# Second layer: values of all three groups for the first half of the tokens ahead of the keys

## The chip, the cores and the metric

The kernel runs on one core of one Trainium2 chip. The metric is device time in microseconds (us), the median of several runs. Engines: TensorE (PE) multiplies matrices, VectorE (DVE), ScalarE (ACT) and GpSimd (POOL) do the elementwise work, SyncE (SP) issues the DMAs. Every engine works through its own queue in order.

## The reference

Two layers over 1024 tokens of width 1024, batch 1, in float32. The first is gated linear attention; its output goes through a layer norm and gives `x1`. The second is attention with three dilated windows (groups) over one shared set of keys and values. What matters here:

```python
def shared_kv(x, w_kv):                  # x is x1, (1, 1024, 1024)
    kv = x @ w_kv
    k, v = jnp.split(kv, [SWA_KV_HALF], axis=-1)
    k = rope(k.reshape(bsz, s, 6, 128), pos)     # 3 groups x 2 heads, rotated by position
    v = v.reshape(bsz, s, 3, 2, 128)
...
x = layer_norm(DEEPNORM_ALPHA * x + y, ln_g[layer], ln_b[layer])   # mean, variance, scale, shift
```

The queries are projected the same way and rotated. Each group then attends within its own window and stride, and the three results are mixed by their softmax weights.

## The kernel before

Everything is kept transposed: 128 features on the partitions, 1024 tokens along the free axis, cut into two halves of 512 tokens. Float32 products are made of three matmuls in a rounded format: each operand is split into a high part (`xh`, `wh`) and a low part (`xl`, `wl`), and `mm3` (L616) adds `wh xh`, `wh xl` and `wl xh`. ACT rounds the high part (`split_hi`), DVE or POOL subtracts to get the low part (`split_lo`).

Weights come through `load_w` (L603): a DMA into `wf` (2 buffers), then `wh` (3 buffers) and `wl` (3 buffers), up to 1024 columns each. Accumulators `acc` have two banks.

`project` (L633) makes one 128-feature piece for one or both halves: 24 matmuls of 512 columns a half (8 slices of the input, three matmuls each). `project_tok` (L642) makes 256 features token by token: it needs two weight pieces, and works in blocks of 128 tokens, each 24 matmuls of 256 columns; the first 12 use the first weight piece, the others the second. The values of a group are made this way, four blocks a half.

Before the second layer starts, `out_ln(0, half)` (L1017) makes `x1` for each half: projection, residual (`rt`), sum over features by ones-matmuls on PE (`ms<-sum,onesr`), subtraction of the mean, squares (`sq`), the second pair of column sums, the scale factor `R` by ACT, then for each of eight slices a product with `R`, a scaling and shift, and the split into `x1h` and `x1l`. The second half's projection is still on PE while the first half is normalised, and the second half is normalised while PE already works for the second layer.

`layer_b` (L1124) starts the second layer. Its order is at L1201 to L1217: values of group 0 for the first half; the six key pieces for the first half; the same six for the second half (weights loaded again), each followed by `rows`, which turns a slice of `x1` with four PE transposes for the end of the program; values of group 0 for the second half; then values of group 1 and of group 2 for all tokens. Each key half piece is rotated on DVE by `rope` (L1134): a product with the cosines (`t<-acc,cosT`), two with the sines, and an addition into `K` (DVE or POOL). Values of groups 1 and 2 go to DRAM (`Vn`, `vd`) and come back in another order (`load_v`). Then query projection and attention follow, head by head.

The text order is not the issue order. `Sched.order` (L249) simulates the program with a cost table and lists, for each engine, the operation that can start first; among equals the one written first wins, with weight loads moved ahead and evacuations of accumulators a little ahead. The order that results is fixed at build time.

Of the kernel before, what the change touches and what calls it, by code (L numbers as in the profile page):

```python
# [575 lines left out]
def trunk(tc, xT, wP, wA, wAv, wa, w2, b2, ng, wO, wK, wV, wB, wOB, lng, lnb,  # L576
# [19 lines left out]
    def page(pool, dt, name):  # L596
        return pool.tile([128, T], dt, name=name, tag="pg", bufs=16)

    def hs(half):
        return slice(half * 512, half * 512 + 512)  # L600


    def load_w(src):  # L603
        with S.later(-WEIGHTS):
            return load_w_now(src)
# [21 lines left out]
    def proj_cols(w, xs, r, acc):  # L627
        hi, lo = w
        for kt in range(NK):
            xh, xl = xs[kt]  # L630
            mm3(acc, hi[:, kt, :], lo[:, kt, :], xh[:, r], xl[:, r], kt)

    def project(piece, xs, evac, halves=(0, 1)):  # L633
        w = load_w(piece)
        for half in halves:
            acc = ps.tile([128, 512], F32, name="acc", bufs=2)
            proj_cols(w, xs, hs(half), acc)
            with S.later(-EVAC):
                evac(half, acc)


    def project_tok(unit, xs, blocks, evac):  # L642
        w = [load_w(unit[:, kh * 4:kh * 4 + 4, :]) for kh in range(2)]
        for j, sel in blocks:
            acc = ps.tile([128, 256], F32, name="acc", bufs=2)
            for kt in range(NK):
                hi, lo = w[kt // 4]
                xh, xl = xs[kt]
                wh, wl = hi[:, kt % 4, :], lo[:, kt % 4, :]
                with S.group():  # L650
                    S.tensor.matmul(acc, sel(xh), wh, start=(kt == 0), stop=False)
                    S.tensor.matmul(acc, sel(xh), wl, start=False, stop=False)
                    S.tensor.matmul(acc, sel(xl), wh, start=False, stop=(kt == NK - 1))
            with S.later(-EVAC):
                evac(j, acc)

    def turn_blocks(dst, blocks):

        n = len(blocks)
        pt = ps.tile([128, 4, 128], F32, name="ms", bufs=2)  # L660
        with S.group():
            for i, b in enumerate(blocks):
                S.tensor.transpose(pt[:, i, :], b, ident)
        S.va.copy(dst, pt[:, :n, :].rearrange("p a b -> p (a b)"))

    def blk(x, j):
        return x[:, j * 128:j * 128 + 128]
# [335 lines left out]
    def small(name, tag, bufs, dt=F32, shape=(128, 512)):  # L1003
        return hp.tile(list(shape), dt, name=name, tag=tag, bufs=bufs)
# [108 lines left out]
    def to_group(pg, g, half):  # L1113
        if g == 2:
            return pg.rearrange("p (e a n) -> p n a e", e=16, a=8)[:, half * 4:half * 4 + 4]
        n = 512 // DIL[g]
        return pg.rearrange("p (r i) -> p i r", r=DIL[g])[:, half * n:half * n + n, :]

    def tok_view(ap, g):
        if g == 2:  # L1120
            return ap.rearrange("p (n a e) -> p n a e", n=4, a=8)
        return ap.rearrange("p (i r) -> p i r", r=DIL[g])

    def layer_b(xs):  # L1124
# [9 lines left out]
        def rope(pg, g, half, acc):  # L1134
            r = hs(half)
            t1 = small("t1", "t1", 2)
            S.vector.tensor_mul(t1, acc, cosT[:, r])
            t2 = small("t2", "t2", 2)
            S.vector.tensor_mul(t2[0:64, :], acc[64:128, :], sinT[64:128, r])
            S.vector.tensor_mul(t2[64:128, :], acc[0:64, :], sinT[0:64, r])  # L1140
            S.vp.tensor_add(to_group(pg, g, half), tok_view(t1, g), tok_view(t2, g))

        K = [[page(p0, F32, f"K{c}{g}") for g in range(3)] for c in range(2)]
        V = [[None] * 3 for _ in range(2)]

        def proj_v0(blocks):
            for c in range(2):
                if V[c][0] is None:
                    V[c][0] = page(p0, F32, f"V{c}0")

            def evac(j, acc):
                S.scalar.activation(blk(V[0][0], j), acc[:, 0:128], AF.Copy)
                S.vector.tensor_copy(blk(V[1][0], j), acc[:, 128:256])
            project_tok(wV[0], xs, [(j, lambda x, j=j: blk(x, j)) for j in blocks], evac)


        def proj_v(g):
            stage = {}

            def evac(j, acc):  # L1160
                if j % 4 == 0:
                    stage[j // 4] = page(p0, F32, "Vn")
                pg = stage[j // 4]
                dst = pg[:, j % 4 * 256:j % 4 * 256 + 256]
                if j % 2:
                    S.scalar.activation(dst, acc, AF.Copy)
                else:
                    S.vector.tensor_copy(dst, acc)
                if j % 4 == 3:
                    h = j // 4 * 512  # L1170
                    rows = pg.rearrange("p (n e) -> p n e", n=4)
                    if g == 1:
                        S.sync.dma_start(vd[h:h + 512, :].rearrange("(n p) e -> p n e", p=128), rows)
                    else:
                        for c in range(2):
                            S.sync.dma_start(vd3[c][h:h + 512, :].rearrange("(n p) e -> p n e", p=128),
                                              rows[:, :, c * 128:c * 128 + 128])
            project_tok(wV[g], xs, [(j, lambda x, j=j: blk(x, j)) for j in range(8)], evac)

        def load_v(c, g):  # L1180
            V[c][g] = page(p0, F32, f"V{c}{g}")
            if g == 1:
                for n in range(2):
                    S.sync.dma_start(
                        V[c][g].rearrange("p (r n e) -> p r n e", r=4, n=2)[:, :, n, :],
                        vd[n * 512:n * 512 + 512, c * 128:c * 128 + 128].rearrange("(p r) e -> p r e", r=4))
            else:

                src = vd3[c].rearrange("(n a s k j) e -> k s a n (j e)", n=8, a=8, s=2, k=2)
                for k in range(2):  # L1190
                    for s in range(2):
                        S.sync.dma_start(V[c][g][k * 64:k * 64 + 64, s * 512:s * 512 + 512], src[k, s])

        def rows(et):
            f, t = small("x1f", "d", 4), small("x1r", "d", 4)
            S.sync.dma_start(f, x1d[et][:, 512:1024])
            turn_blocks(t, [blk(f, i) for i in range(4)])
            for i in range(4):
                S.sync.dma_start(x1t[i][:, et * 128:et * 128 + 128], blk(t, i))

        proj_v0(range(4))  # L1201
        for half in range(2):
            for g in range(3):
                for c in range(2):
                    project(wK[2 * g + c], xs, lambda hf, acc, p=K[c][g]: rope(p, g, hf, acc), (half,))
                    if half:
                        rows(2 * g + c)
        proj_v0(range(4, 8))
        rows(6)
        rows(7)  # L1210
        proj_v(1)
        load_v(0, 1)
        proj_v(2)
        load_v(0, 2)
        for g in range(3):
            S.sync.dma_start(kvd[g], K[1][g])
        S.sync.dma_start(kvd[3], V[1][0])  # L1217
# [252 lines left out]
    for half in range(2):  # L1470
        out_ln(0, hs(half), lambda et: load_w(wO[et]), lambda et: xT[et * 128:et * 128 + 128, :], emit_a)
    U = layer_b(x1s)

    ogs.clear()
# [118 lines left out]
```

## Time and profile before

| | |
|---|---|
| median of 3 runs | 1194.42 us (1194.0 to 1195.4) |
| the profiled execution | 1194.93 us, of which the trace's span is 1193.1 us |
| PE | busy 1173.8 us (98%) |
| DVE | busy 760.7 us (64%) |
| ACT | busy 477.4 us (40%) |
| POOL | busy 191.9 us (16%) |

The span is the time from the first to the last recorded instruction; the remaining 1.8 us lie around it. A matmul counts as busy from its start to its modelled end, and matmuls overlap, so the distance between the starts of two neighbours (the pitch) tells more than the duration. All times in the rows are counted from the span's start.

### The profile page before, as it was taken

What the parts mean: (1) busy time and instruction counts of PE and PEld (TensorE: products, weight loads), DVE (VectorE), ACT (ScalarE), POOL (GpSimd) and SP (SyncE); (2) the same over time, 40 slices, a digit from 0 to 9 for tenths busy, and PEclk for the clock granted to TensorE, in tenths of its full rate; (3) what the DMA queues carried; (4) which work ended last, traced back from release to release, by engine and by line L of the source; (5) the groups of instructions that cost most, each with busy time, mean ns of one, the idle gap of its engine ahead of it and who ended that gap; (6) DMA issues with size and microseconds to landing.
All of it is one profiled execution on the core that took longest, in us unless ns stands there. A gap on an engine that the chain in (4) does not pass through costs nothing.

```text
span 1193.1 us, 20435 instructions
## 1 busy us (share of the span) xinstructions
PE 1173.8 (98%) x8220; PEld 1006.7 (84%) x8220; DVE 760.7 (64%) x1448; ACT 477.4 (40%) x1000; POOL 191.9 (16%) x126
## 2 busy tenths in 40 slices
PE   9999999999999998999999999999999999999997
PEld 7898988988988887879988888888888888888885
DVE  6482962953977598972155747565746675747578
ACT  5352533534454344332115352525244336345242
POOL 0011101211222122331010302020203022203000
PEclk9999999999999999999999999999999999999999
DMA  8102111121243454375231111121242110224544
GB/s 258 51 20 71 37 55 53 38 70 37 70 168 101 138 199 135 133 213 177 89 107 37 39 52 37 37 54 36 55 142 40 52 38 19 55 73 125 172 145 176
DMA packets 93232, 107.52 MB, mean 90 GB/s; under 512 B 44017, under 2 KB 62321, under 8 KB 93137
## 3 DMA queue, kind: packets, MB, share of 16 engines
q1 hardware_dynamic: 93136, 106.22, 28.4%
q8 instruction: 64, 1.05, 0.4%
q14 instruction: 32, 0.25, 0.1%
HBM read 85.02 MB, written 21.17 MB: 89 GB/s over the span
## 4 chain that ended last, share of the span: by engine, by line
PE 92%; DVE 5%; issue 1%; ACT 1%; DMA 1%; SPq 0%; POOL 0%; DVEq 0%; ACTq 0%; POOLq 0%
PE acc L441 66%; PE po L441 10%; PE lv L441 9%; PE ms L441 4%; PE pro L441 3%; DVE X L441 2%; DVE t L441 1%; DVE oT L441 1%; DMA xf<-in_xT 1%; DVE rt L441 0%; DVE K L441 0%; ACT wh L441 0%; DVE b L441 0%; DVE sum L441 0%; DVE x1l L441 0%
## 5 line engine op out<-in xcount | busy, mean ns | idle before, releaser
L441 PE MATMUL acc<-x1h,wh 128*128 128x512 f32 x608 | 251.8, 414 | 1.7 <-DVE t L441 1.7
L441 PE MATMUL acc<-x1l,wh 128*128 128x512 f32 x608 | 238.0, 391 | 0.2 <-DVE x1l L441 0.2
L441 PE MATMUL acc<-x1h,wl 128*128 128x512 f32 x608 | 238.1, 392 | 0.0
L441 ACT ACTIVATE wh<-wf 128x1024 fp32r<-128x1024 f32 (+2 forms) x102 | 106.1, 1042 | 265.4 <-PE acc L441 201.1
L441 POOL TENSOR_TENSOR wl<-wf,wh 128x1024 fp32r<-128x1024 f32 x45 | 108.0, 2400 | 607.2 <-ACT wh L441 573.5
L441 PEld LDWEIGHTS acc<-x1h,wl 128*128 128x128 f32 x608 | 114.6, 189 | 24.7
L441 PEld LDWEIGHTS acc<-x1h,wh 128*128 128x128 f32 x608 | 114.9, 189 | 24.0 <-DVE t L441 2.4
L441 PEld LDWEIGHTS acc<-x1l,wh 128*128 128x128 f32 x608 | 115.0, 189 | 22.2 <-DVE x1l L441 0.8
L441 DVE TENSOR_TENSOR wl<-wf,wh 128x1024 fp32r<-128x1024 f32 (+2 forms) x57 | 74.2, 1301 | 64.7 <-ACT wh L441 64.3
L441 ACT ACTIVATE P<-P,sts 128x128 f32<-128x128 f32 (+2 forms) x192 | 81.2, 425 | 45.1 <-DVE sts L441 44.2
L441 DVE TENSOR_TENSOR t<-acc,cosT 128x512 f32<-128x512 f32 x60 | 41.4, 690 | 71.4 <-PE acc L441 71.3
L441 DVE TENSOR_TENSOR t<-acc,sinT 64x512 f32<-64x512 f32 x120 | 82.6, 688 | 1.8 <-ACT R L441 0.2
L441 PE MATMUL acc<-xh,wh 128*128 128x512 f32 x208 | 82.5, 397 | 0.0
L441 PE MATMUL acc<-xh,wl 128*128 128x512 f32 x208 | 81.1, 390 | 0.0
L441 PE MATMUL acc<-xl,wh 128*128 128x512 f32 x208 | 81.0, 389 | 0.0
L441 PE MATMUL acc<-wh,xh 128*128 128x256 f32 x256 | 75.6, 295 | 0.0
L441 DVE TENSOR_TENSOR Q<-t,t 128x512 f32<-128x512 f32 x48 | 71.4, 1488 | 1.6
L441 DVE CUSTOM_DVE_ANT_0 P<-lv,bmask 128x256 f32<-128x256 f32 (+1 forms) x128 | 47.5, 381 | 39.0 <-PE lv L441 37.9
L441 PE MATMUL acc<-wl,xh 128*128 128x256 f32 x256 | 72.3, 282 | 0.0
L441 PE MATMUL acc<-wh,xl 128*128 128x256 f32 x256 | 72.3, 282 | 0.0
L441 PE MATMUL lv<-K,Q 128*64 128x64 f32 (+2 forms) x512 | 68.3, 286 | 0.0
L441 PE MATMUL po<-PT,V 64*128 64x64 f32 (+2 forms) x592 | 68.2, 293 | 0.0
(229 smaller groups left out, 2351.6 us busy)
## 6 DMA issues: line engine op xcount, KB each, us to landing
wf<-in_wB SPq DMA_DIRECT2D x32, 512.0 KB
wf<-in_wO SPq DMA_DIRECT2D x16, 512.0 KB
wf<-in_wOB SPq DMA_DIRECT2D x16, 512.0 KB
wf<-in_wA SPq DMA_DIRECT2D x13, 512.0 KB
wf<-in_wK SPq DMA_DIRECT2D x12, 512.0 KB
wf<-in_wAv SPq DMA_DIRECT2D x8, 512.0 KB
res<-in_xT SPq DMA_DIRECT2D x16, 256.0 KB
wf<-in_wV SPq DMA_DIRECT2D x8, 512.0 KB
```

The costliest lines, as they stand in the source:

```text
L441: getattr(handle[o.eng], meth)(*[conv(a) for a in args], **{k: conv(v) for k, v in kw.items()})
```

## The change

`proj_v` takes a half, so that groups 1 and 2 are made in two calls. The first half of the tokens now has its values of all three groups made first. Then each key piece is made for both halves from one weight load, followed by `rows`. Then come the values of groups 1 and 2 for the second half, `rows(6)` and `rows(7)`, and the values of group 0 for the second half.

```diff
-        def proj_v(g):
+        def proj_v(g, half):
...
-            project_tok(wV[g], xs, [(j, lambda x, j=j: blk(x, j)) for j in range(8)], evac)
+            project_tok(wV[g], xs, [(j, lambda x, j=j: blk(x, j)) for j in range(half * 4, half * 4 + 4)], evac)
...
         proj_v0(range(4))
-        for half in range(2):
-            for g in range(3):
-                for c in range(2):
-                    project(wK[2 * g + c], xs, lambda hf, acc, p=K[c][g]: rope(p, g, hf, acc), (half,))
-                    if half:
-                        rows(2 * g + c)
-        proj_v0(range(4, 8))
+        for g in (1, 2):
+            proj_v(g, 0)
+        for g in range(3):
+            for c in range(2):
+                project(wK[2 * g + c], xs, lambda hf, acc, p=K[c][g]: rope(p, g, hf, acc))
+                rows(2 * g + c)
+        for g in (1, 2):
+            proj_v(g, 1)
+            load_v(0, g)
         rows(6)
         rows(7)
-        proj_v(1)
-        load_v(0, 1)
-        proj_v(2)
-        load_v(0, 2)
+        proj_v0(range(4, 8))
```

PE, the second pair of column sums (`ms<-sum,onesr`, the variance of the second half). `acc` is an accumulator, `x1h0` to `x1h7` are the high parts of the eight slices of `x1`, the numbers behind an underscore count buffers. Before:

```order
L441 MATMUL acc_4782<-x1h7_4583,wh_4720 128x512
L441 MATMUL acc_4782<-x1l7_4597,wh_4720 128x512
L441 MATMUL acc_4782<-x1h7_4583,wl_4734 128x512
L441 MATMUL ms_4838<-sum_4828,onesr_193 128x512
L441 MATMUL ms_4838<-sum_4832,onesr_193 128x512
L441 MATMUL acc_4848<-x1h0_4416,wh_4740 128x512
```

And now:

```order
L441 MATMUL acc_4876<-wh_4861,x1h4_4502 128x256
L441 MATMUL acc_4876<-wl_4874,x1h4_4502 128x256
L441 MATMUL acc_4876<-wh_4861,x1l4_4517 128x256
L441 MATMUL ms_4903<-sum_4869,onesr_193 128x512
L441 MATMUL ms_4903<-sum_4888,onesr_193 128x512
L441 MATMUL acc_4876<-wh_4861,x1h5_4533 128x256
```

The sums stood behind the second key half piece; they now stand 15 matmuls into the first block of the values of group 2.

DVE, from the low split of that sum (`sum<-sq2,sum`) to the first slices of the layer norm's end. `t1` and `t2` are the rotary products, `rt` the rows that are normalised, `R` their scale factor. Before:

```order
L441 TENSOR_TENSOR t1_4826<-acc_4782,cosT_4553 128x512
L441 TENSOR_TENSOR sum_4832<-sq2_4700,sum_4828 128x512
L441 TENSOR_TENSOR t2_4836<-acc_4736,sinT_4557 64x512 x2
L441 TENSOR_TENSOR K00_4846<-t1_4787,t2_4836 128x512
L441 TENSOR_TENSOR t2_4852<-acc_4782,sinT_4557 64x512 x2
L441 TENSOR_TENSOR K10_4861<-t1_4826,t2_4852 128x512
L441 TENSOR_TENSOR rt_4242<-rt_4242,R_4844 128x512
L441 TENSOR_SCALAR rt_4242<-rt_4242,lngc_124,lnbc_128 128x512
```

And now:

```order
L441 COPY Vn_4780<-acc_4806 128x256
L441 TENSOR_TENSOR wl_4874<-wf_4750,wh_4861 128x1024
L441 TENSOR_TENSOR sum_4888<-sq2_4700,sum_4869 128x512
L441 TENSOR_TENSOR wl_4896<-wf_4782,wh_4880 128x1024
L441 COPY Vn_4925<-acc_4876 128x256
L441 TENSOR_TENSOR rt_4242<-rt_4242,R_4919 128x512
L441 TENSOR_SCALAR rt_4242<-rt_4242,lngc_124,lnbc_128 128x512
```

The rotary steps are gone from this part of the queue; value copies and weight splits stand there. The first rotary step now stands behind the last product with `R`.

PE, the first matmuls that read the second half of `x1`. Before, they open the second round of key pieces (`acc_5015`, the first piece again), behind all six first-half pieces (`acc_4973` is the sixth):

```order
L441 MATMUL acc_4973<-x1h7_4583,wh_4892 128x512
L441 MATMUL acc_4973<-x1l7_4597,wh_4892 128x512
L441 MATMUL acc_4973<-x1h7_4583,wl_4909 128x512
L441 MATMUL acc_5015<-x1h0_4416,wh_4937 128x512
L441 MATMUL acc_5015<-x1l0_4424,wh_4937 128x512
```

Now they follow the first half of the first key piece (`acc_5028`), with the same weights:

```order
L441 MATMUL acc_5028<-x1h7_4583,wh_4880 128x512
L441 MATMUL acc_5028<-x1l7_4597,wh_4880 128x512
L441 MATMUL acc_5028<-x1h7_4583,wl_4896 128x512
L441 MATMUL acc_5077<-x1h0_4416,wh_4880 128x512
L441 MATMUL acc_5077<-x1l0_4424,wh_4880 128x512
```

Between the end of the second half's projection and this place PE has three value units and one key half piece, where it had one value unit and six key half pieces. From the query projection on, every engine's order is what it was.

## Rows read from the trace of the kernel before

**Rows 1.** The page, part 2: PE's busy tenths in 40 equal slices.
```profile
PE   9999999999999998999999999999999999999997
```

**Rows 2.** PE timeline, 448 to 598: start, duration, operation, [idle before <-releaser].
```profile
448.71 0.28 PE L441 MATMUL acc<-wh,x1h 128*128 128x256 f32 x1
...
455.90 0.90 PE L441 MATMUL ms<-sum,onesr 128*128 128x512 f32 x2
456.64 0.28 PE L441 MATMUL acc<-wh,x1h 128*128 128x256 f32 x1
...
460.96 0.40 PE L441 MATMUL acc<-x1h,wh 128*128 128x512 f32 x1
...
471.64 0.39 PE L441 MATMUL acc<-x1h,wl 128*128 128x512 f32 x1
473.47 0.49 PE L441 MATMUL ms<-sum,onesr 128*128 128x512 f32 x1 [1.44 <-ACT sum L441]
475.92 0.80 PE L441 MATMUL ms<-sum,onesr 128*128 128x512 f32 x1 [1.96 <-DVE sum L441]
477.35 0.79 PE L441 MATMUL acc<-x1h,wh 128*128 128x512 f32 x1 [0.63 <-DVE t L441]
...
482.12 0.39 PE L441 MATMUL acc<-x1h,wl 128*128 128x512 f32 x1
...
504.13 0.60 PE L441 MATMUL ms<-ident,x1f 128*128 128x128 f32 x4
504.49 0.48 PE L441 MATMUL acc<-x1h,wh 128*128 128x512 f32 x1
...
515.79 0.50 PE L441 MATMUL acc<-x1h,wh 128*128 128x512 f32 x1 [1.05 <-DVE t L441]
...
597.52 0.40 PE L441 MATMUL acc<-x1h,wh 128*128 128x512 f32 x1
```

**Rows 3.** Stretches: length, busy (count) of PE, PEld, DVE, ACT, POOL, PEclk, DMA.
```profile
472.00:476.00 4.00, 0.60 (x3) 0.27 (x2) 3.59 (x4) 1.41 (x2) 2.35 (x1) 0.90 0.00 0
476.00:480.00 4.00, 3.37 (x7) 2.36 (x8) 3.72 (x6) 1.32 (x2) 0.00 (x0) 0.50 0.35 131
...
557.01:597.52 40.51, 40.51 (x340) 40.51 (x339) 5.52 (x10) 6.24 (x11) 0.00 (x0) 1.00 0.34 103
```

**Rows 4.** DVE timeline, columns as in rows 2.
```profile
460.81 1.23 DVE L441 TENSOR_TENSOR wl<-wf,wh 128x1024 fp32r<-128x1024 f32 x1
...
473.45 2.42 DVE L441 TENSOR_TENSOR sum<-sq,sum 128x512 fp32r<-128x512 f32 x1 [0.38 <-ACT sum L441]
...
480.24 0.69 DVE L441 TENSOR_TENSOR rt<-rt,R 128x512 f32<-128x512 f32 x1
...
512.12 0.69 DVE L441 TENSOR_TENSOR x1l<-rt,x1h 128x512 fp32r<-128x512 f32 x1 [1.49 <-ACT x1h L441]
```

**Rows 5.** DVE groups from 448.71 to 513, rotary steps: xcount | busy, mean ns.
```profile
L441 DVE TENSOR_TENSOR K<-t,t 128x512 f32<-128x512 f32 x6 | 10.1, 1684 | 0.2
L441 DVE TENSOR_TENSOR t<-acc,sinT 64x512 f32<-64x512 f32 x12 | 8.3, 688 | 0.3 <-ACT R L441 0.2
...
L441 DVE TENSOR_TENSOR t<-acc,cosT 128x512 f32<-128x512 f32 x6 | 4.1, 690 | 2.1 <-PE acc L441 2.0
```

**Rows 6.** POOL timeline, columns as in rows 2.
```profile
472.97 2.35 POOL L441 TENSOR_TENSOR wl<-wf,wh 128x1024 fp32r<-128x1024 f32 x1 [5.13 <-ACT wh L441]
483.43 1.60 POOL L441 TENSOR_TENSOR x1l<-rt,x1h 128x512 fp32r<-128x512 f32 x1 [8.11 <-ACT x1h L441]
```

**Rows 7.** Instructions that write Vn: durations ns (min/median/max), first and last start.
```profile
L441 DVE COPY Vn<-acc x8: 425/425/426, 554.1 to 594.8; 128x256 f32<-128x256 f32 x8
```

**Rows 8.** ACT timeline, columns as in rows 2.
```profile
459.72 1.06 ACT L441 ACTIVATE wh<-wf 128x1024 fp32r<-128x1024 f32 x1
...
476.82 0.69 ACT L441 ACTIVATE t<-ms,epsc 128x512 f32<-128x512 f32 x1 [3.40 <-PE ms L441]
477.54 0.63 ACT L441 ACTIVATE R<-t 128x512 f32<-128x512 f32 x1
```

## The prediction

> **What bounds the kernel now.** I read the page first. TensorE (PE) is busy for at least nine tenths of 38 of the 40 slices of the span [rows 1], so a new order of the same matmuls can return only two things: time in which PE waits, and time in which its matmuls run slowly. One of the two other slices is the last; the 8 covers 447 to 477 us, and there the second layer begins, with the key and value projections from 448.71 to 597.52 us [rows 2]. There I read PE's timeline row by row, then the rows of VectorE (DVE), ScalarE (ACT) and GpSimd (POOL) that PE waits for.
>
> The first-half tokens of the normalised activations x1 are there from 448.71 on; those of the second half go through their layer norm while PE works on the first half. The pitch of PE's work comes from [rows 2]. The first value unit, 96 matmuls of 256 columns, takes 460.96 - 448.71 less 0.74 for the pair of column sums between 455.90 and 456.64: 11.51 us, 0.120 each. Key matmuls of 512 columns take (504.13 - 482.12) / 97 = 0.227 each, so a half piece of 24 takes 5.45. A group of four transposes takes 504.49 - 504.13 = 0.36.
>
> PE loses time in two stretches:
> - 471.64 to 482.12, 10.48 us. The work in it is 12 key matmuls (2.72) and the two column sums of the variance (0.74). Lost: **7.0**. Of this 4.03 is idle (1.44 and 1.96 before the sums, 0.63 before the next piece). The 11 matmuls from 477.35 to 482.12 then take 4.77 where 2.50 is their pitch, 2.3 more; the granted clock of 476 to 480 is 0.50, the lower of the two levels, 1.2 GHz [rows 3].
> - 504.13 to 515.79, 11.66 us. The work is 36 matmuls (8.17) and three transpose groups (1.08). Lost: **2.4**. PE has caught up with the layer norm of the second half here (its last low part is written at 512.12 [rows 4]) and then waits 1.05 us for DVE to empty an accumulator [rows 2].
>
> Together 9.4 us. From 557.01 to 597.52 PE is busy for all 40.51 us [rows 3]: the other value units cost nothing beyond their pitch.
>
> Why the sums come late: DVE. The rotary steps of the six first-half key pieces cost it 10.1 + 8.3 + 4.1 = 22.5 us between 448.71 and 513 [rows 5], in the same in-order queue as the layer norm. And the DVE step that PE waits for, the split of the squares' sum, takes 2.42 us instead of 0.69 [rows 4], while POOL runs a weight split of 2.35 us [rows 6].
>
> I book the slow clock with the gap ahead of it. The Trainium skill, "TensorE: Matmul & The Clock Gate", Part 1, calls the throttled state the default, which activity releases. By that rule the slow stretch goes when the gap goes, as here, where it follows the longest gap and no other piece of the stage is slow; if it did not, the gain would be 2.3 us smaller.
>
> **The change part by part.** Matmul counts stay: the same value and key matmuls, the same transposes. Two of the twenty weight loads in this stage go (twelve key loads become six, eight value loads become twelve): about 1 us of ACT and 1.2 to 2.4 us of a splitter each, on engines with idle time, so 0 on the path. The DMAs move with their steps; the values of groups 1 and 2 go to DRAM and back further ahead of their use.
>
> What the move does is change which work covers the layer norm. Before, PE had one value unit and six key half pieces (11.5 + 32.7 = 44.2 us) before it touched the second half. Now it has three value units and one key half piece (34.5 + 5.45 = 40.0). The cover is 4.2 us shorter, but the rotary steps leave it, and four copies of 0.43 us [rows 7] come in. So DVE has some 20 us less to do while it normalises.
>
> On PE without waits: unit V0 ends at 460.96 as before, V1 at 472.48, V2 at 484.74 (with 0.74 for the sums), the first half of the first key piece at 490.19, its second half at 495.64. I walk the other queues against these places with durations of the rows.
> - *Second weight piece of V1.* Needed 12 matmuls into V1, at 462.4. The DVE split that writes it stands in the same place of the queue as before and ended at 460.81 + 1.23 = 462.04 [rows 4]. In time by 0.4.
> - *Second weight piece of V2.* Its buffer comes free 12 matmuls before the end of V1, at 471.04. Rounding on ACT 1.06 [rows 8], split on DVE 1.23: 473.4 with handovers. Needed at 473.9. In time by about 0.5.
> - *Sums of the variance.* They now stand 15 matmuls into V2, at 474.3. The last square is added on POOL at about 472 (after four subtractions and three adds of 0.69 that no rotary step interrupts); ACT's part follows at 472.9, behind the weight rounding; DVE's part at 473.4 + 0.69 = 474.1. POOL has nothing to do then, so I take 0.69, not 2.42. On time, or late by 0.2.
> - *Scale factor R.* Sums end at 475.0; ACT needs 0.69 + 0.63 [rows 8]. DVE's first multiplication by R can start at about 476.8, against 480.24 [rows 4].
> - *Rest of the layer norm.* DVE has 18 steps of at most 0.69 (eight products, five scalings, five splits), two weight splits of 1.23 and one copy of 0.43: 15.3 us at most, nearer 14 since they overlap. It also waits about 1 us for a weight buffer that PE frees in the last block of V2. It ends at 491.6 to 493.1. Two ACT steps of about 0.7 and the last split on POOL, 1.60 [rows 6], follow: 494.6 to 496.1. PE needs that piece in the last triple of the second key half, at 490.19 + 21 x 0.227 + 0.23 = 495.2. So 0 to 0.9 late; I take 0.4. The same count on the old queue (480.24, its 20 steps, four rotary groups, its waits) ends at 512, where the trace has 512.12.
> - *The later hand-overs*, V1 to V2 and V2 to V0 of the second half, meet an idle DVE, as those in the 40.51 us without a gap [rows 3]. I take 0.2 for both.
> - The new wait at the second key half stands at the head of PE's queue, with all keys and values behind it; it is priced above. The rotary steps of the keys now come one piece per 5.45 us behind the layer norm, with 3.75 us of DVE each (22.5 / 6).
>
> Sum against the profiled execution, 1194.93 us: - 9.4 + 0.2 (sums) + 0.2 (weights in the first half) + 0.4 + 0.2 = 1186.5. The median of the runs is 0.5 lower, so **1186.0**. If nothing is late it is 1185.0; a new order of waits could give back no more than the 9.4, so the low end is that less the 0.6 by which runs differ.
>
> **The rivals.** All are against the median 1194.4.
> - *Weight hand-overs between value units.* Four units now follow another value unit at half the length (two did). If ACT or DVE is held up by the layer norm, or the split falls to POOL (2.35), each is 1.06 + 2.35 against 2.88 available, some 0.8 late with semaphores: 3.2 for four, 1189.2 with the other residues. For it: the slack is 0.4. Against it: the new order has all four on DVE.
> - *The end of the layer norm is late by several us*, with slow matmuls after the gap. If the 4.2 us of shorter cover came through in full: 4.2 and 2.3 for the clock against 9.4 returned, with the other residues 1192.1, nearly no gain. Short of that, POOL's last two splits now run beside DVE's first rotary addition. Beside POOL a DVE step took 2.42 for 0.69, 1.7 more [rows 4]; that much on the last piece gives 1187.7. The Trainium skill, "GPSIMD Engine Reference", Key points, states that GpSimd shares its SBUF interfaces with VectorE and contends with instructions that read two SBUF inputs; by that rule the 1.7 is to be expected, and the trace's 2.42 agrees.
> - *Slower: the layer norm is no earlier than it was.* If it is not the rotary steps that hold it but its own chain across three engines, the last piece still lands at 512.8. PE then stands from 495.2 on, 17.6 us, and 2.3 more for the clock, against 9.4 returned: 1204.9. It decides from a last piece at about 502. Against it: DVE is the engine with the rotary steps, and its idle time in that stretch is small.
> - *The change does nothing*, because the time goes elsewhere (later stages wait for V): 1194. The 9 in every slice after the sixteenth, but for the last [rows 1], leaves little to lose there.
>
> **How the numbers follow.** Forecast (1184.4 to 1188): 0.62. Hand-overs and a small delay (to 1191.5): 0.20. Late by some us, or nothing gained (1192 to 1196.8): 0.10. Slower: 0.06. Under 1184.4: 0.02. A difference under 0.2%, 2.4 us, can't be told from none. So faster 0.84, same 0.10, slower 0.06; the range is 1184.4 to 1191.5.
>
> **What would show it.** Right: no row of PE with idle time ahead of the second pair of sums; granted clock 1.00 from 470 to 500; DVE's first product with R near 477; the last low part of x1 near 495; the first query matmul at 588 to 589 instead of 597.52. Wrong: a gap on PE at the second block of a value unit (weights), or at the second key half (layer norm), with matmuls at the lower clock behind it.

## The result, and the profile after

The changed kernel takes 1185.31 us (median of 6 runs, 1184.79 to 1186.68), the kernel before 1194.95 us on the same chip (6 runs, 1194.0 to 1195.77). The ratio is 0.9921, 95% interval 0.9909 to 0.9933: 9.6 us faster. The profiled execution took 1185.19 us with a span of 1183.0.

The page of the kernel after, part 2, PE's busy tenths, which answers to [rows 1]. The 8 at the 16th digit is gone:

```profile
PE   9999999999999999999999999999999999999997
```

PE's timeline of the kernel after (start, duration, operation), against [rows 2]. First the start of the stage, then the second pair of column sums and the matmul behind it, the last triple of the first key piece's second half, and the first query matmul:

```profile
448.58 0.28 PE L441 MATMUL acc<-wh,x1h 128*128 128x256 f32 x1
...
474.12 0.63 PE L441 MATMUL ms<-sum,onesr 128*128 128x512 f32 x2
474.58 0.28 PE L441 MATMUL acc<-wh,x1h 128*128 128x256 f32 x1
...
494.52 0.39 PE L441 MATMUL acc<-x1h,wh 128*128 128x512 f32 x1
494.75 0.39 PE L441 MATMUL acc<-x1l,wh 128*128 128x512 f32 x1
494.98 0.39 PE L441 MATMUL acc<-x1h,wl 128*128 128x512 f32 x1
...
588.17 0.40 PE L441 MATMUL acc<-x1h,wh 128*128 128x512 f32 x1
```

None of these rows has a bracket with idle time. The two sums stand together, while before the first waited 1.44 us and the second 1.96. The stage from the first value matmul to the first query matmul is 588.17 - 448.58 = 139.59 us long; it was 148.81. All that PE still waits for between 440 and 600 us is one line (in total, times, longest, us):

```profile
PE ms L441 <- DMA x1f<-x1d: 0.2, 1, 0.2
```

The same two stretches as in [rows 3], kernel after (length, busy time and count of PE, PEld, DVE, ACT and POOL, granted clock, DMA). PE is busy throughout, at the full clock; before, it was busy for 0.60 and 3.37 of 4 us and the second stretch ran at 0.50:

```profile
472.00:476.00 4.00, 4.00 (x33) 3.91 (x33) 3.11 (x4) 3.06 (x6) 0.00 (x0) 1.00 0.33 86
476.00:480.00 4.00, 4.00 (x36) 4.00 (x35) 3.93 (x8) 1.79 (x5) 0.00 (x0) 1.00 1.00 352
```

DVE's timeline of the kernel after, against [rows 4]: the split of the variance's sum, the first product with R, and the last one with the first rotary step behind it:

```profile
473.31 0.68 DVE L441 TENSOR_TENSOR sum<-sq,sum 128x512 fp32r<-128x512 f32 x1
...
476.20 0.68 DVE L441 TENSOR_TENSOR rt<-rt,R 128x512 f32<-128x512 f32 x1
...
489.99 0.68 DVE L441 TENSOR_TENSOR rt<-rt,R 128x512 f32<-128x512 f32 x1
490.60 0.68 DVE L441 TENSOR_TENSOR t<-acc,cosT 128x512 f32<-128x512 f32 x1
```

The split takes 0.68 us instead of 2.42. The last low part of x1 is written by POOL (kernel after, POOL's timeline, against [rows 6]); it is there at 492.28 + 1.29 = 493.57, and PE reads it at 494.75, 1.2 us later:

```profile
492.28 1.29 POOL L441 TENSOR_TENSOR x1l<-rt,x1h 128x512 fp32r<-128x512 f32 x1 [0.15 <-ACT x1h L441]
```

### The profile page after: what moved, and what is told of

The parts are those of the page before. It is cut to its first block, busy times and chain, and to the rows that moved or that the text cites. A ratio compares the mean times of both kernels' runs of the same rounds, so it can differ in the third digit from the quotient of the medians.

```text
span 1183.0 us, 20411 instructions
## 1 busy us (share of the span) xinstructions
PE 1170.7 (99%) x8220; PEld 1005.8 (85%) x8220; DVE 758.8 (64%) x1447; ACT 475.2 (40%) x998; POOL 185.5 (16%) x125
## 4 chain that ended last, share of the span: by engine, by line
PE 93%; DVE 4%; issue 1%; DMA 1%; ACT 1%; SPq 0%; POOL 0%; DVEq 0%; ACTq 0%; POOLq 0%
PE acc L441 66%; PE po L441 10%; PE lv L441 9%; PE ms L441 4%; PE pro L441 4%; DVE X L441 2%; DVE oT L441 1%; DMA ogf<-ogA 1%; DMA x1f<-x1d 0%; ACT wh L441 0%; SPq L441 0%; DVE wl L441 0%; DVE b L441 0%; DVE Dg L441 0%; DVE rt L441 0%
## 5 line engine op out<-in xcount | busy, mean ns | idle before, releaser
L441 POOL TENSOR_TENSOR wl<-wf,wh 128x1024 fp32r<-128x1024 f32 x40 | 96.0, 2399 | 593.0 <-ACT wh L441 559.2
L441 DVE TENSOR_TENSOR wl<-wf,wh 128x1024 fp32r<-128x1024 f32 (+2 forms) x60 | 77.9, 1299 | 67.1 <-ACT wh L441 66.5
```

Of the source, the lines that this page charges most:

```text
L441: getattr(handle[o.eng], meth)(*[conv(a) for a in args], **{k: conv(v) for k, v in kw.items()})
```

## The experiments

The prediction says that the time was lost because VectorE's queue held rotary steps beside the layer norm of the second half. Rivals: the length of the work that covers the layer norm counts alone, or the key weights' loading, or the step of VectorE that takes 2.42 us beside GpSimd, or the two accumulators that wait for their rotary steps. Times are medians; each ratio is to the kernel before in the same set of runs (medians 1195.29 for the first four, 1195.16 for the next four, 1194.87 for the last two).

| run | us | ratio, 95% interval |
|---|---|---|
| e1_norope | 1184.79 | 0.9912 [0.9897, 0.9927] |
| e2_vfirst_ksplit | 1184.81 | 0.9917 [0.9902, 0.9932] |
| e3_kmerge | 1198.80 | 1.0033 [1.0021, 1.0044] |
| e4_dveload | 1210.84 | 1.0132 [1.0116, 1.0147] |
| e5_twoV | 1191.55 | 0.9970 [0.9958, 0.9982] |
| e6_addpool | 1196.70 | 1.0012 [1.0003, 1.0022] |
| e7_halfrope | 1186.32 | 0.9923 [0.9909, 0.9938] |
| e8_poolsplit | 1189.37 | 0.9950 [0.9935, 0.9965] |
| e9_dvesplit | 1192.69 | 0.9979 [0.9969, 0.9989] |
| e10_accout | 1191.42 | 0.9974 [0.9964, 0.9983] |

**The old order without the rotary steps (e1, e7).**

```diff
+            if half == 0 and any(pg is K[c][q] for c in range(2) for q in range(3)):
+                S.scalar.activation(to_group(pg, g, half), tok_view(acc, g), AF.Copy)
+                return
```

e7 does the same for `K[0][0]`, `K[0][1]` and `K[0][2]` alone.

> The order of before, but the six first-half key pieces get no rotary steps: one ACT copy each instead (their rotation is left out, so the keys of the first half are unrotated). Theory, that the rotary steps on DVE delayed the layer norm: most of the 9.4 us comes back without any new order, 1185 to 1188, and the 2.42 us split of the squares' sum and the gaps ahead of it are gone or under 1 us. Rival, that the order of values and keys or the doubled key loads cost the time: 1193 to 1195, gaps as before.

> The order of the kernel before; three of the six first-half key pieces (head 0 of each group) are only copied out by ScalarE, without their rotary steps, so half of the 22.5 us of VectorE's rotary work is gone. It is a dose between the kernel before and the run without any of the six: by my theory the sums of the variance come 2 to 4 us earlier and the time is 1186 to 1191 us. If the 2.42 us step beside GpSimd's split and not the load makes the gap, the time is 1192 or more.

e1 gives 1184.79 us, as fast as the changed kernel and 0.2 under my range, in the old order. PE's timeline of e1 at the second pair of sums shows no gap:

```profile
472.11 0.39 PE L441 MATMUL acc<-x1h,wl 128*128 128x512 f32 x1
472.34 0.63 PE L441 MATMUL ms<-sum,onesr 128*128 128x512 f32 x2
472.81 0.39 PE L441 MATMUL acc<-x1h,wh 128*128 128x512 f32 x1
```

e7, which leaves out half of the rotary steps, gives 1186.32, and PE waits for nothing in the stage. So the whole 9.4 us hang on what the six rotary groups do, and three of them less are already enough. But both runs change three things at once: VectorE has fewer rotary steps, the accumulators are emptied by ScalarE at once, and the order, which is built anew from costs, moves weight splits from GpSimd to VectorE (GpSimd's first weight split in the stage starts at 484.81 us in e1 and at 499.13 in e7, before at 472.97). VectorE's busy time as a whole hardly falls in e7: 28.9 us of the 32 from 476 to 508 us, before 29.2. The next three runs take these apart as far as they can.

**The old order, rotary additions on GpSimd (e6).**

```diff
-            S.vp.tensor_add(to_group(pg, g, half), tok_view(t1, g), tok_view(t2, g))
+            eng = S.vp
+            if half == 0 and any(pg is K[c][q] for c in range(2) for q in range(3)):
+                eng = S.gpsimd
+            eng.tensor_add(to_group(pg, g, half), tok_view(t1, g), tok_view(t2, g))
```

> The order of the kernel before; the last rotary step (the addition) of the six first-half key pieces is put on GpSimd instead of VectorE, which takes up to 10.1 us of the 22.5 us off VectorE in the stretch. By my theory about half of the lost 9.4 us comes back or more: 1186 to 1191 us. By the rival that a GpSimd step beside VectorE slows VectorE as much as it relieves it (2.42 us for 0.69 in the kernel before), the time stays at 1193 to 1196.

1196.70 us: my expectation of 1186 to 1191 missed, the rival's 1193 to 1196 is near, and it is even 0.12% slower than before. VectorE's groups between 476 and 508 us (count, busy us, mean ns, idle before) show where the 10.1 us went. Before:

```profile
L441 DVE TENSOR_TENSOR K<-t,t 128x512 f32<-128x512 f32 x6 | 10.1, 1684 | 0.2
...
L441 DVE TENSOR_TENSOR rt<-rt,R 128x512 f32<-128x512 f32 x7 | 4.8, 680 | 0.0
...
L441 DVE TENSOR_TENSOR x1l<-rt,x1h 128x512 fp32r<-128x512 f32 x4 | 2.7, 682 | 0.0
```

And in e6:

```profile
L441 DVE TENSOR_TENSOR rt<-rt,R 128x512 f32<-128x512 f32 x7 | 9.2, 1311 | 0.0
...
L441 DVE TENSOR_TENSOR x1l<-rt,x1h 128x512 fp32r<-128x512 f32 x5 | 7.3, 1458 | 0.3
```

The additions are gone from VectorE, but its products with R take 1311 ns instead of 680 and its low parts 1458 instead of 682: 4.4 us and, with one low part more, 4.6 us come back. Busy time moved to GpSimd was paid again on VectorE. One pair of rows of e6 (VectorE's timeline, then GpSimd's) shows how: VectorE's product starts beside GpSimd's addition, which ends at 487.89 + 1.77 = 489.66, and ends 0.54 us after it, at 490.20.

```profile
488.41 1.79 DVE L441 TENSOR_TENSOR rt<-rt,R 128x512 f32<-128x512 f32 x1
```

```profile
487.89 1.77 POOL L441 TENSOR_TENSOR K<-t,t 128x512 f32<-128x512 f32 x1
```

The first gap is untouched as well (1.44 and 1.96 us ahead of the sums), because no addition stands ahead of the sums at all. VectorE's timeline of the kernel before, around the split at 473.45 [rows 4]:

```profile
466.62 0.69 DVE L441 TENSOR_TENSOR t<-acc,cosT 128x512 f32<-128x512 f32 x1
...
472.38 0.68 DVE L441 TENSOR_TENSOR t<-acc,cosT 128x512 f32<-128x512 f32 x1
...
475.90 1.39 DVE L441 TENSOR_TENSOR t<-acc,sinT 64x512 f32<-64x512 f32 x2
```

Only two cosine products, 1.37 us, precede the sums. The sine products of the first key piece come behind them and end at 477.29, and until then its accumulator is held: the third key piece, which needs it, starts at 477.35 [rows 2]. My sentence that 22.5 us of rotary steps make the sums late is therefore wrong for this gap.

**The old order, contention at the sum taken away (e9).** Key weights of the first half are split on VectorE alone (the line that chooses the engine; the rest of the diff only hands it on).

```diff
...
-        w = load_w(piece)
+        w = load_w(piece, S.vector if halves == (0,) else None)
```

> The order of the kernel before; the low-part splits of the key weights of the first half are all put on VectorE, so GpSimd does nothing beside VectorE's split of the variance's sum. It takes the contention away and leaves the rotary load. The split of the sum should take 0.69 us instead of 2.42, behind a weight split of 1.23 that now stands ahead of it: the sums come about 1 us earlier, and the rotary additions lose the microsecond that GpSimd costs them, against 1.23 more for each weight split. By my theory (the load decides, the contention is a small part of it) the time is 1192 to 1196 us. By the rival that the 2.42 us step makes the gap and the slow matmuls behind it, 1190 or less.

1192.69 us: as the theory of the load expected, which only says that the meeting with GpSimd is not all of it. The split of the sum takes 0.69 us, behind the weight split that now stands ahead of it (VectorE's timeline of e9):

```profile
473.23 1.22 DVE L441 TENSOR_TENSOR wl<-wf,wh 128x1024 fp32r<-128x1024 f32 x1
474.37 0.69 DVE L441 TENSOR_TENSOR sum<-sq,sum 128x512 fp32r<-128x512 f32 x1
```

PE's timeline of e9 shows what is left of the gap: 1.44 + 0.90 + 0.92 us, where it was 4.03.

```profile
473.71 0.50 PE L441 MATMUL ms<-sum,onesr 128*128 128x512 f32 x1 [1.44 <-ACT sum L441]
475.11 0.50 PE L441 MATMUL ms<-sum,onesr 128*128 128x512 f32 x1 [0.90 <-DVE sum L441]
476.53 0.50 PE L441 MATMUL acc<-x1h,wh 128*128 128x512 f32 x1 [0.92 <-DVE t L441]
```

Two splits have changed sides against the kernel before: the one beside the sum's split, and the next, which GpSimd started at 486.26 and VectorE starts at 485.33 in e9. Together they were worth about 2.2 us, a quarter of the loss; the run doesn't separate them.

**The old order, accumulators freed at once, rotary steps kept (e10).**

```diff
+            if half == 0 and any(pg is K[c][q] for c in range(2) for q in range(3)):
+                kc = small("kc", "a", 13)
+                S.scalar.activation(kc, acc, AF.Copy)
+                acc = kc
```

> The order of the kernel before; each first-half key accumulator is first copied to SBUF by ScalarE and rotated from there by the same VectorE steps. The accumulator is free at once, VectorE's load is unchanged. It tells whether TensorE's 5.5 us standstill comes only from the two accumulators that wait in VectorE's queue for their rotary steps, or from the load itself. If only the accumulators: the standstill and the slow matmuls go and 7 us come back, 1186 to 1189 us. By my theory of the load, TensorE goes on but reaches the second half 7 us sooner while the layer norm still ends at 508 to 512 us, so it waits there instead: 1191 to 1196 us.

1191.42 us, in the range of the load theory, at its lower end; the rival's 1186 to 1189 missed. PE's timeline of e10:

```profile
475.86 0.63 PE L441 MATMUL ms<-sum,onesr 128*128 128x512 f32 x2
...
496.41 0.50 PE L441 MATMUL acc<-x1l,wh 128*128 128x512 f32 x1 [0.65 <-DVE x1l L441]
...
501.74 0.50 PE L441 MATMUL acc<-x1l,wh 128*128 128x512 f32 x1 [1.87 <-DVE x1l L441]
...
512.24 0.50 PE L441 MATMUL acc<-x1h,wh 128*128 128x512 f32 x1 [1.07 <-DVE t L441]
```

The first gap is gone, although VectorE finishes the split of the sum at 475.28 us, hardly earlier than before (475.87): with the accumulator free PE has the third key piece to work on, and the built order puts 4 us of it ahead of the sums. So what held PE in the first gap was an accumulator in VectorE's queue. Then PE reaches the second half's low parts too early and waits for them, 2.5 us, with granted clocks of 0.80 and 0.78 from 500 to 508.

The edit moved more than the accumulators, though. In the kernel before GpSimd made five weight splits between 472 and 505 us; in e10 they stand on VectorE, and GpSimd is idle for 48 us (e10, GpSimd's timeline):

```profile
511.06 4.73 POOL L441 TENSOR_TENSOR wl<-wf,wh 128x1024 fp32r<-128x1024 f32 x2 [47.96 <-ACT wh L441]
```

VectorE is busy for 31.4 of the 32 us from 476 to 508 in e10, for 29.2 before and for 25.7 in the changed kernel. So the second wait shows a VectorE that is late with the low parts, but not that the rotary steps alone make it late.

**The new order with the keys loaded twice (e2).** Keys half by half as before, behind the three value units.

```diff
-        for g in range(3):
-            for c in range(2):
-                project(wK[2 * g + c], xs, lambda hf, acc, p=K[c][g]: rope(p, g, hf, acc))
-                rows(2 * g + c)
+        for half in range(2):
+            for g in range(3):
+                for c in range(2):
+                    project(wK[2 * g + c], xs, lambda hf, acc, p=K[c][g]: rope(p, g, hf, acc), (half,))
+                    if half:
+                        rows(2 * g + c)
```

> The new order, but each key piece is again made half by half with its weights loaded twice (six first halves, then six second halves); only the three value units stand ahead of them. Theory: as the changed kernel, 1185.3 within 1 us, since the layer norm is over before the second halves are wanted and the six added loads lie beside PE. Rival, that one load per key piece is what gained: 1189 to 1195.

1184.81 us, the same as the changed kernel. The saved loads are worth nothing here; putting the values first is all of the gain.

**One or two value units in front instead of three (e3, e5).** e3 keeps only group 0 in front of keys made for both halves:

```diff
-        for half in range(2):
-            for g in range(3):
-                for c in range(2):
-                    project(wK[2 * g + c], xs, lambda hf, acc, p=K[c][g]: rope(p, g, hf, acc), (half,))
-                    if half:
-                        rows(2 * g + c)
+        for g in range(3):
+            for c in range(2):
+                project(wK[2 * g + c], xs, lambda hf, acc, p=K[c][g]: rope(p, g, hf, acc))
+                rows(2 * g + c)
```

e5 has groups 0 and 1 in front and group 2 whole behind the keys (first lines of the diff):

```diff
-        for g in (1, 2):
-            proj_v(g, 0)
+        proj_v(1, 0)
...
```

> The other part of the change alone: one value unit, then each key piece for both halves from one load; groups 1 and 2 at the end as before. Cover of the layer norm is 11.5 + 5.45 us. Theory, that cover counts beside DVE's load: PE stands at the second half of the first key pieces from about 472 to about 485 to 490, with the lower clock behind it: 1198 to 1206. Rival, that only the rotary steps matter: they come late here, so 1185 to 1190.

> Two value units (groups 0 and 1) stand in front, then each key for both halves from one load; group 2 follows whole at the end. The layer norm is still free of rotary steps, but the cover in front of the second key half is two value units and one key half, 23.0 + 0.7 + 5.45 us, so that half is wanted at about 484 us. By my theory (both the rotary load and the length of the cover count) the layer norm's low parts come at about 490 to 493, and TensorE waits 3 to 7 us with slow matmuls behind it: 1189 to 1196 us, against 1185 for the changed kernel. By the rival that only the rotary load counts, 1187 or less.

1198.80 and 1191.55 us, both as expected: the cover counts too. e3 on PE (timeline), the sums and the first matmul of the second half:

```profile
470.96 1.52 PE L441 MATMUL ms<-sum,onesr 128*128 128x512 f32 x2 [4.68 <-ACT sum L441]
475.95 0.80 PE L441 MATMUL acc<-x1h,wh 128*128 128x512 f32 x1 [3.47 <-ACT x1h L441]
```

Here PE has nothing left but work that needs the layer norm. In e5 the sums come without a gap, and what PE waits for between 440 and 600 us (in total, times, longest) is mostly another accumulator: the layer norm's last low parts are written at 491.87 us, PE's next matmuls run until 492.71, VectorE waits 0.88 us for them before it takes its rotary products, and PE goes on at 494.89, when the products are done:

```profile
PE acc L441 <- DVE t L441: 2.2, 1, 2.2
PE acc L441 <- DVE x1l L441: 0.6, 1, 0.6
PE acc L441 <- POOL x1l L441: 0.5, 1, 0.5
```

**The new order with VectorE's load put back (e4).** Eight products of 128x256 behind each first-half block of groups 1 and 2, 27.5 us in all.

```diff
+                if j < 4:
+                    tmp = small("t1", "t1", 2)
+                    for _ in range(8):
+                        S.vector.tensor_mul(tmp[:, 0:256], dst, dst)
```

> The changed kernel with work added on DVE in the cover: eight products of 128x256 behind each of the eight first-half blocks of groups 1 and 2 (64, about 22 to 25 us, results thrown away), about as much as the rotary steps cost. Theory: the layer norm ends 15 to 20 us later, the gain is gone and more, since the cover is 4.2 us shorter than before: 1195 to 1204. Rival, that the gain came from the order of the matmuls or the fewer loads: 1185 to 1188.

1210.84 us: in the expected direction and above the expected range. PE waits 12.4 us for the sums:

```profile
PE ms L441 <- ACT sum L441: 12.4, 1, 12.4
PE acc L441 <- ACT x1h L441: 3.5, 1, 3.5
PE acc L441 <- ACT Vn L441: 1.9, 2, 1.4
```

The granted clock is 0.50 from 500 to 508. I had reckoned with a load near the old 22.5 us and with the layer norm alone; accumulators are emptied late as well (the third line). The new order is not immune: it gains because its values cost VectorE little.

**The new order, value weights split on GpSimd (e8).** The rival of the hand-overs (the line that chooses the engine; the rest of the diff only hands it on).

```diff
...
-        w = [load_w(unit[:, kh * 4:kh * 4 + 4, :]) for kh in range(2)]
+        w = [load_w(unit[:, kh * 4:kh * 4 + 4, :], S.gpsimd) for kh in range(2)]
```

> The changed kernel, with the low-part splits of all value weights put on GpSimd instead of where the scheduler puts them. It measures the rival of the weight hand-overs: rounding 1.06 and a split of 2.35 to 2.40 against 2.88 us of TensorE work in between, 0.6 to 0.8 us late at each of the four hand-overs between value units, and the sum's split of 0.69 may again run beside GpSimd and take up to 2.4. By that price the time is 1187 to 1190 us, with a wait at the second block's weights of every value unit that follows another. If the hand-overs have more room than I counted, it stays at 1185 to 1186.

1189.37 us, a number that I expected, for a reason that I did not. PE's waits in the stage are these (e8, 440 to 600 us):

```profile
PE acc L441 <- ACT x1h L441: 0.8, 1, 0.8
PE acc L441 <- DVE x1l L441: 0.8, 1, 0.8
PE acc L441 <- DVE V L441: 0.3, 1, 0.3
```

All three lie between 453 and 457 us, in the first value unit, where GpSimd's splits stand beside the end of the first half's layer norm; a granted clock of 0.66 from 456 to 460 follows. Of the hand-overs two show, with 0.2 us each between two matmuls that should follow each other (477.32 and 477.65, 569.42 and 569.74, pitch 0.12). The price of 0.8 us for each was too high.

## Why the prediction was right, and where not

Predicted 1186.0 us in 1184.4 to 1191.5, measured 1185.31.

- *What bounds the kernel; 9.4 us lost.* Right: the stage is 9.2 us shorter, 9.4 less the one wait of 0.2. The other 0.5 us by which the two profiled executions differ (9.74 in all) lie outside the stage and are less than the runs of one kernel differ (1194.0 to 1195.77 before).
- *Slow clock booked with the gap.* Right: 1.00 from 470 to 500, and e10, without the first gap, runs at 1.00 from 476 to 484 too. But what the clock costs does not follow the length of the gap: the two stretches from 476 to 484 run at 0.50 and 0.75 before (4.03 us idle), at 0.68 and 0.90 in e6 (4.33 idle) and at 0.67 and 0.91 in e9 (3.26 idle). The rule that the prediction took from the Trainium skill, "TensorE: Matmul & The Clock Gate", Part 1, that activity releases the throttled state, fits these rows.
- *Why the sums come late.* The step that failed. The 22.5 us were one lump of "load"; the runs show several parts. The two weight splits on GpSimd, one of them beside the sum's split, are worth 2.2 us (e9). The two accumulators held for rotary steps keep PE in the rest of the first gap (e10, where the sums are ready as late as before and PE doesn't wait). When the second half's low parts are there decides the rest (e10, the waits at 496 and 501 us); how much of that the rotary steps make by themselves is not shown, since e10 also puts five weight splits on VectorE. The changed kernel takes the rotary steps out of this stretch altogether and so did not need them told apart: the sum came out right although this step was not. For e6, which removes 10.1 us of load and neither of the first two parts, the lump gave a wrong forecast. How much a third accumulator would give in the old order was not tried.
- *Sums of the variance at 474.3, split 0.69.* Right: PE starts them at 474.12 without a gap, so the assumed 0.2 did not arise. The split ends at 473.99 us; in the old order it ended at 475.87, and at 475.06 and 475.28 in e9 and e10. So the sums come 1.9 us earlier; the rest of the gap closes because PE reaches them 2.2 us later (at 474.12, in the old order one pitch after 471.64), with value matmuls to run until then.
- *R at 476.8.* 476.20; the pair of sums holds PE for 0.46 us, not 0.74, when the second does not wait.
- *End of the layer norm, 494.6 to 496.1 against a need of 495.2; 0.4 assumed.* Too dark: 493.57 against 494.75. VectorE was through at 490.67 instead of 491.6 to 493.1, since it started 0.6 us earlier and the wait of about 1 us for a weight buffer did not come. GpSimd's last split took 1.29 us, not 1.60: VectorE's step at that moment reads an accumulator.
- *Hand-overs, 0.2 and 0.2.* None; even with GpSimd's longer split none costs more than 0.2 (e8). V2's second weight piece was written at 473.40, as worked out.
- *Weight loads at nothing.* Right (e2).
- *Cover 4.2 us shorter but enough.* Right, by 1.2 us: with 11.5 us less of it the gain falls from 9.6 to 3.6 (e5), with another 11.5 less it becomes a loss (e3).

## What to carry to other kernels

A wait of TensorE for an in-order engine has two prices, the value that comes late and the accumulator that is not emptied; look which matmul could have run meanwhile and what holds its bank before putting the whole wait down to load. As cover for a chain on VectorE take the TensorE work whose outputs cost VectorE least (here 0.43 us for a value block that it copies, 2.88 us on TensorE, against 3.75 for a rotated key half, 5.45 on TensorE). Moving two-input steps from VectorE to GpSimd can return nothing, since VectorE's own two-input steps wait for it: count both engines in the same stretch after the move.

## What was new about the hardware

VectorE's steps with two operands in SBUF don't run slowly beside GpSimd: they end a fixed time after GpSimd's instruction ends, as if they waited for it and then ran. For a step that takes 0.69 us alone this is 0.54 to 0.56: in e6 490.20 against 489.66 (above); in the kernel before, the split of the sum ends at 475.87 and GpSimd's weight split at 475.32 [rows 4, 6]. For a rotary addition that takes 1.10 us alone (in the changed kernel at 514.80) it is 0.94: 489.60 against 488.66 in the kernel before (VectorE's timeline, then GpSimd's).

```profile
487.42 2.18 DVE L441 TENSOR_TENSOR K<-t,t 128x512 f32<-128x512 f32 x1
```

```profile
486.26 2.40 POOL L441 TENSOR_TENSOR wl<-wf,wh 128x1024 fp32r<-128x1024 f32 x1 [1.22 <-ACT wh L441]
```

The scaling and shift, with one operand tile in SBUF, is held too: in e6 one takes 1.38 us instead of 0.55 and ends at 481.28, 0.28 after GpSimd's addition. A step that reads one operand from an accumulator is not held: in e6 the two sine products beside a weight split of 2.41 us take 0.69 each.

```profile
490.81 1.39 DVE L441 TENSOR_TENSOR t<-acc,sinT 64x512 f32<-64x512 f32 x2
```

```profile
490.92 2.41 POOL L441 TENSOR_TENSOR wl<-wf,wh 128x1024 fp32r<-128x1024 f32 x1 [1.27 <-ACT wh L441]
```

The Trainium skill, "SBUF — State Buffer", SBUF: two separate sides, says that the port pair which the two engines share is held for a whole instruction and the loser blocks entirely; the rows agree. By that rule the price of 1.7 us that I carried for one meeting was no constant: it is what is left of GpSimd's instruction when VectorE arrives (here 1.87 us at 473.45), less about 0.15.
